# A Tile kernel on one core: high priority for the inverses of the triangular blocks and their merging

## The chip, the cores and the metric

The kernel runs on one core of one Trainium2 chip. The metric is the device time of one execution in microseconds; a kernel's time is the median of its runs. The engines are named as in the profile: PE is TensorE's matmul and PEld its weight load, DVE is VectorE, ACT is ScalarE, POOL is GpSimd, and SP is SyncE, which issues nearly all DMAs here.

## The reference

The reference is a trunk of two layers over 512 positions of width 1024. The first layer mixes tokens by an RWKV-7 recurrence, the second by a gated spatial unit, and a SwiGLU FFN stands behind each. The change touches the recurrence alone. For each of 16 heads of width 64 it is

```python
def step(S, inp):
    r_t, w_t, k_t, v_t, a_t, b_t = inp
    sa = jnp.einsum('bhij,bhj->bhi', S, a_t)
    S = (S * w_t[:, :, None, :]
         + sa[..., None] * b_t[:, :, None, :]
         + v_t[..., None] * k_t[:, :, None, :])
    y = jnp.einsum('bhij,bhj->bhi', S, r_t)
    return S, y
```

Its output y then goes through a norm per head, a bonus term, an output gate g and the product with w_o:

```python
    return (y * g) @ w_o
```

## The kernel before, in words

**The recurrence in chunks.** The 512 positions are cut into 8 chunks of 64. Within a chunk the steps depend on each other through a 64x64 lower triangular matrix per chunk and head, and the kernel inverts these matrices, so that a chunk becomes a few matrix products. The 16 heads are worked through in four blocks of four heads, called blocks 0 to 3. For each block b there are the steps

- E (`early`): decays, keys and gates; writes the operands to DRAM (sa, sb);
- F (`front`, L673 to L728): loads them back as ST and MV; PE forms the chunk products `lm` (L709); ACT and DVE copy their parts to LA (L715, the triangular matrices), MV (L712) and BX (L716); transposes `bkt` (L722) and four more copies to BX (L726, L727);
- B (`back`, L730 to L817), in which the change lies, described below;
- S (`scan`): for each chunk the state products `us` and `Yp` (L843, L856), the new state su on DVE and ACT (L847, L849), and loads of `su` on SP (L828);
- N (`finish`): the norm per head with mean mu (L879 to L901), the gates (L904 to L920) with loads g2 and g2r and the small DVE step g2x (L912), the transposes yt (L927), the product ob (L928), and the store of ob to `od` (L936) on SP, two for each of blocks 0 to 2.

**The step B.** First the inverses of the 32x32 diagonal blocks: LX is the transposed LA (L735, DVE), POOL masks LA in place (`LAs`, L738), and a recursion of 15 steps on DVE, each a product tm (L744) and an addition to Dm (L746), inverts 16x16 blocks. Steps are told apart below by the width of their tile: the seventh product is `128x2x63`, the eighth `128x128`, the ninth `128x2x63` again. Two DVE transposes give Dn and Dt (L749, L750). Then PE transposes MV to MVt (`mvt`, L751 to L760; ACT copies). Then the merging, first to 32x32 and then to 64x64: Qp (L766, PE, 64 small products of 32x32), Qs (DVE), Np and Tp (L775, L778, PE), copies of Np to Dn2 by ACT and of Tp to bdT by ACT and DVE (L783), Q2p (L789, PE), its copies to Q2 (L792 ACT, L793 DVE), T2p (L798, PE) and its copies to bdT (L802, ACT and DVE). Last, for each of four units, the product mp (L807, PE) with its ACT copy (L809), and two products gh (L814, PE), each with a pair of additions on DVE into MV (L816, L817).

**The end of the mixer.** The output product `acc` (L156 to L158, from `out_proj`) takes its left operand oT from ob: for k below 6 SP loads a pair of od back as `oraw` (L980), ACT rounds it to oT (L131) and DVE forms the rest (L132). Blocks 0 to 2 supply three such loads, and the first products acc are already run while block 3 is still in its step B.

**What sets the order.** The code is written in the order of PLAN (L33):

```python
PLAN = "P0 E0 P1 P2 E1 P3 E2 E3 X0 F0 B0 F1 V0 V1 V2 V3 B1 S0 F2 S1 F3 N0 B2 N1 B3 S2 N2 S3 N3".split()
```

so block 2's step B comes behind block 3's step F and block 0's step N. But that isn't the order in which an engine runs its instructions: the kernel is built with a scheduler (`schedule_with_timeline_sim=True`, L1135) that goes through the instructions with a modelled timeline and puts each engine's queue in order by priority, which without further words follows the code. It may pull an instruction forward where it models the engine as free. PSUM banks are shared by tags (`BANKS_RWKV`, L29), so an instruction that writes a bank waits until the former tile in it has been read; gh, Qp, Np, Tp, Q2p and T2p turn over the two banks of the tag `pt`.

Of the kernel before, what the change touches and what calls it, by code (L numbers as in the profile page):

```python
# [82 lines left out]
class Trunk:  # L83
# [287 lines left out]
    def rwkv(self, x0, nxt):  # L371
# [3 lines left out]
        with ExitStack() as ctx:  # L375
# [14 lines left out]
            def e2(name, shape=(P, 2, T), dt=F32):  # L390
                return rp.tile(list(shape), dt, name=name, tag="e2", bufs=E2)
# [338 lines left out]
            def back(b, o):  # L730

                MV, BX, LA, Dm = (o[n] for n in ("MV", "BX", "LA", "Dm"))
                LX = e2("LX", (P, 2, 528))

                v.transpose(full(LX), LA.rearrange("p q c (x t) -> p t (q c x)", x=2))  # L735
                LAu = LA.rearrange("p q c t -> p (q c) t")
                LAs = LA.rearrange("p q c (x t) -> p (q c) x t", t=16)
                g.tensor_tensor(LAs, LAs, m16.unsqueeze(1).unsqueeze(3).broadcast_to([P, 16, 4, 16]), op=ALU.mult)  # L738
                LXd, Dmd = diag(LX), diag(Dm)
                for j in range(15):  # L740
                    n = 15 - j
                    tm = rp.tile([P, 2, 64], F32, name="tm", tag="tm", bufs=1)
                    tv = tm[:, :, 0:n * (j + 1)].rearrange("p b (i c) -> p b i c", c=j + 1)
                    v.tensor_tensor(tv, LXd[:, :, j + 1:16, j:j + 1].broadcast_to([P, 2, n, j + 1]),  # L744
                                    Dmd[:, :, j:j + 1, 0:j + 1].broadcast_to([P, 2, n, j + 1]), op=ALU.mult)
                    v.tensor_tensor(Dmd[:, :, j + 1:16, 0:j + 1], Dmd[:, :, j + 1:16, 0:j + 1], tv, op=ALU.add)  # L746
                Dt = rp.tile([P, 16, 2, 32], F32, name="Dt", tag="hid", bufs=1)
                Dn = self.sm.tile([P, 16, 2, 32], F32, name="hn", tag="hn", bufs=2)
                v.transpose(Dn.rearrange("p u x s -> p s (u x)"), full(Dm).rearrange("p t s -> p s t"))  # L749
# [14 lines left out]
                for u in range(16):  # L764
                    for z, hd, x in quarters:
                        mm(Qp[z:z + 32, u * 32:(u + 1) * 32], LAu[z:z + 32, u, 32 * x:32 * x + 32], Dn[z:z + 32, u, x, :],  # L766
                           start=True, stop=True)
                Qs = el("Qs", (P, 16, 32))
                v.tensor_tensor(Qs, Qp.rearrange("p (u s) -> p u s", s=32), id32.unsqueeze(1).broadcast_to([P, 16, 32]), op=ALU.add)
                Np = self.bank("pt", "Np")  # L770
                Tp = self.bank("pt", "Tp")
                for u in range(16):
                    for z, hd, x in quarters:
                        if x == 0:
                            mm(Np[z:z + 32, u * 32:(u + 1) * 32], Dt[z:z + 32, u, x, :], Qs[z:z + 32, u, :], start=True, stop=True)  # L775
                for u in range(16):
                    for z, hd, x in quarters:
                        mm(Tp[z:z + 32, u * 32:(u + 1) * 32], Qs[z:z + 32, u, :], Dt[z:z + 32, u, x, :], start=True, stop=True)  # L778
                Dn2 = el("Dn2", (P, 16, 32))
                for z in (0, 64):  # L780
                    a.copy(Dn2[z:z + 32].rearrange("p u s -> p (u s)"), Np[z:z + 32, :])
# [357 lines left out]
```

## Time and profile before

| | |
|---|---|
| median of 3 runs | 1424.7 us (1423.27 to 1425.45) |
| the profiled execution | 1426.41 us, its span 1424.7 us |
| granted clock of PE, mean | 0.962 |
| busy share of PE, DVE, ACT, POOL | 94%, 56%, 40%, 19% |
| instructions | 21481 |
| DMA | 143.04 MB, mean 100 GB/s |

The span is the profiled execution from its first instruction to its last; all times below count from its start. PE is busy 94% of it. The page cuts the span in 40 slices of some 36 us, and the slices that are less full are at the start and around slices 5, 9 and 12 (180 to 470 us), where the recurrence is. The profile's line numbers are those of the kernel before; in the changed kernel they are 1 higher from L735 to L760 and 2 higher from L762 on.

### The profile page before, as it was taken

To read this page: it belongs to the slowest core of one execution; us is meant where nothing else is said; L and a number is where in the kernel's file an instruction comes from. 1 tells how busy PE (TensorE), PEld (TensorE's weight loads), DVE (VectorE), ACT (ScalarE), POOL (GpSimd) and SP (SyncE) were. 2 spreads that over 40 slices of the span, in tenths; PEclk is the share of its full clock that TensorE was granted. 3 is DMA by queue.
4 is the path that set the end of the run, shared out by engine and by line. 5 is a ranking of instruction groups with operands and counts; after the bars stand their busy time and mean duration, and the time that the engine had idled before them with its cause. 6 is when DMAs were issued, how large, how long until landed. Compare 5 with 4: busy or idle time off the path is not lost.

```text
span 1424.7 us, 21481 instructions
## 1 busy us (share of the span) xinstructions
PE 1338.3 (94%) x8472; PEld 1091.2 (77%) x8472; DVE 791.8 (56%) x1318; ACT 569.1 (40%) x1060; POOL 274.5 (19%) x248
## 2 busy tenths in 40 slices
PE   5899997987889979999999999999999999999998
PEld 3576686976768768888888888778888888888886
DVE  6962776388685775554544222865575455443223
ACT  5654665363723363323322122743363232322221
POOL 6154463133311231111111000210121111110000
PEclk9999998987969989999999999999999999999999
DMA  5133467351322423333332232343213333332331
GB/s 157 30 107 92 127 182 200 94 150 43 87 65 88 130 90 104 89 89 103 90 99 94 89 118 74 104 129 109 89 52 112 103 89 89 103 90 103 89 96 67
DMA packets 210324, 143.04 MB, mean 100 GB/s; under 512 B 59664, under 2 KB 185136, under 8 KB 210224
## 3 DMA queue, kind: packets, MB, share of 16 engines
q1 hardware_dynamic: 208544, 135.90, 32.2%
q0 software_dynamic: 1680, 5.77, 1.3%
q8 instruction: 67, 1.10, 0.3%
q14 instruction: 33, 0.27, 0.1%
HBM read 125.39 MB, written 14.16 MB: 98 GB/s over the span
## 4 chain that ended last, share of the span: by engine, by line
PE 77%; DVE 7%; ACT 2%; issue 2%; DMA 2%; POOL 1%; SPq 1%; DVEq 0%; POOLq 0%; ACTq 0%
PE gu L158 12%; PE gu L156 12%; PE gu L157 12%; PE acc L156 8%; PE acc L157 8%; PE acc L158 8%; PE gh L814 2%; PE lm L709 2%; PE u L156 1%; PE u L158 1%; PE u L157 1%; PE Yp L856 1%; PE mp L807 1%; PE proj L158 1%; PE proj L156 1%
## 5 line engine op out<-in xcount | busy, mean ns | idle before, releaser
L131 ACT CAST whi<-wraw 128x1024 fp32r<-128x1024 f32 x161 | 168.8, 1050 | 472.5 <-PE gu L157 257.2
L132 DVE TENSOR_TENSOR wlo<-wraw,whi 128x1024 fp32r<-128x1024 f32 x161 | 246.6, 1532 | 197.2 <-ACT whi L131 193.2
L157 PE MATMUL gu<-hT,whi 128*128 128x512 f32 (+1 forms) x768 | 289.6, 378 | 4.4 <-DVE hT L59 4.4
L156 PE MATMUL gu<-hT,whi 128*128 128x512 f32 (+1 forms) x768 | 290.2, 380 | 0.8 <-ACT hT L57 0.8
L158 PE MATMUL gu<-hT,wlo 128*128 128x512 f32 (+1 forms) x768 | 289.7, 378 | 0.0
L157 PEld LDWEIGHTS gu<-hT,whi 128*128 128x128 f32 x768 | 146.0, 190 | 34.0 <-DVE hT L59 4.7
L156 PEld LDWEIGHTS gu<-hT,whi 128*128 128x128 f32 x768 | 145.8, 191 | 29.5 <-ACT hT L57 1.0
L158 PEld LDWEIGHTS gu<-hT,wlo 128*128 128x128 f32 x768 | 145.8, 190 | 29.0 <-issue 0.2
L157 PE MATMUL acc<-wlo,act 128*128 128x512 f32 x416 | 163.9, 394 | 0.0
L156 PE MATMUL acc<-whi,act 128*128 128x512 f32 x416 | 163.6, 394 | 0.0
L158 PE MATMUL acc<-whi,act 128*128 128x512 f32 x416 | 160.5, 394 | 0.0
L333 POOL TENSOR_TENSOR sg<-sg,hn 128x512 f32<-128x512 f32 x44 | 56.7, 1288 | 422.5 <-DVE sg L332 422.5
L332 DVE TENSOR_TENSOR sg<-sg,gu 128x512 f32<-128x512 f32 x44 | 30.2, 687 | 142.5 <-PE gu L158 141.1
L148 POOL TENSOR_TENSOR wlo<-wraw,whi 128x1024 fp32r<-128x1024 f32 x28 | 70.1, 2505 | 169.9 <-ACT whi L147 151.1
L158 PEld LDWEIGHTS acc<-whi,act 128*128 128x128 f32 x416 | 78.2, 188 | 18.1
L156 PEld LDWEIGHTS acc<-whi,act 128*128 128x128 f32 x416 | 78.2, 188 | 18.0
L157 PEld LDWEIGHTS acc<-wlo,act 128*128 128x128 f32 x416 | 78.1, 188 | 18.0
L330 DVE TENSOR_TENSOR sg<-gu,hn 128x512 f32<-128x512 f32 x44 | 30.4, 691 | 67.8 <-PE gu L158 67.6
L131 ACT CAST act<-sg 128x512 fp32r<-128x512 f32 x52 | 32.3, 622 | 72.2 <-POOL sg L333 58.1
L158 PE MATMUL proj<-xsp,wlo 128*128 128x512 f32 x128 | 53.7, 421 | 0.0
L156 PE MATMUL proj<-xsp,whi 128*128 128x512 f32 x128 | 51.9, 405 | 0.4 <-ACT k L529 0.4
L709 PE MATMUL lm<-MV,ST 128*128 128x128 f32 x256 | 41.6, 316 | 11.2 <-DMA ST<-sb 7.9
(305 smaller groups left out, 2248.8 us busy)
## 6 DMA issues: line engine op xcount, KB each, us to landing
wraw<-in_ffn_w_gate_dram SPq DMA_DIRECT2D x44, 512.0 KB, 3.6
wraw<-in_ffn_w_up_dram SPq DMA_DIRECT2D x44, 512.0 KB
wraw<-in_ffn_w_down_dram SPq DMA_DIRECT2D x44, 512.0 KB, 3.6
wraw<-in_rwkv_w_rkv_dram SPq DMA_DIRECT2D x24, 512.0 KB, 3.5
wraw<-in_sgu_w_in_dram SPq DMA_DIRECT2D x16, 512.0 KB, 3.6
x<-in_x_dram SPq DMA_DIRECT2D x8, 512.0 KB, 3.7
MV<-sa SPq DMA_DIRECT2D x64, 64.0 KB, 2.6
ST<-sb SPq DMA_DIRECT2D x8, 512.0 KB, 4.5
```

The source lines that it names most:

```text
L131: self.nc.scalar.copy(hi, src)
L132: self.nc.vector.tensor_tensor(lo, src, hi.bitcast(F32), op=ALU.subtract)
L148: nc.gpsimd.tensor_tensor(lo, raw, hi.bitcast(F32), op=ALU.subtract)
L156: mm(out, lhs[0], rhs[0], start=start, stop=False)
L157: mm(out, lhs[0], rhs[1], start=False, stop=False)
L158: mm(out, lhs[1], rhs[0], start=False, stop=stop)
L330: nc.vector.tensor_tensor(sg, pp[0], yb, op=ALU.mult)
L332: nc.vector.tensor_tensor(sg, sg, pp[1], op=ALU.mult)
L333: nc.gpsimd.tensor_tensor(sg, sg, yb, op=ALU.mult)
L709: mm(lm[:, cc * P:(cc + 1) * P], st[:, cc].rearrange("p n t -> p (n t)"), mv[:, :, cc, hd, :], start=True, stop=True)
L807: mm(mp[:, cc * P:(cc + 1) * P], bdT[:, q * NC + 4 * hh + cc].rearrange("p h t -> p (h t)"), mt[:, cc, :], start=True, stop=True)
L814: mm(gh[:, cc * P:(cc + 1) * P], mt[rows, cc, :], bx[rows, 0:2, cc, :], start=True, stop=True)
```

## The change

The change wraps two parts of `back` in `with tc.high_priority():`, which tells the scheduler to place the instructions inside ahead of all that is ready outside. The first part runs from LX to the transposes Dn and Dt, the second from Qp to the copies of T2p. The transposes MVt between them stay outside, as do mp, gh and the additions behind them. Nothing is computed otherwise. The diff, without the lines that are only indented:

```diff
             def back(b, o):
 
                 MV, BX, LA, Dm = (o[n] for n in ("MV", "BX", "LA", "Dm"))
-                LX = e2("LX", (P, 2, 528))
-
-                v.transpose(full(LX), LA.rearrange("p q c (x t) -> p t (q c x)", x=2))
...
-                v.transpose(Dt.rearrange("p u x t -> p t (u x)"), full(Dm))
+                with tc.high_priority():
+                    LX = e2("LX", (P, 2, 528))
+
+                    v.transpose(full(LX), LA.rearrange("p q c (x t) -> p t (q c x)", x=2))
...
+                    v.transpose(Dt.rearrange("p u x t -> p t (u x)"), full(Dm))
                 MVt = {}
                 for hh in range(2):
...
-                quarters = [(64 * hd + 32 * x, hd, x) for hd in q2 for x in q2]
-                Qp = self.bank("pt", "Qp")
...
-                    cp(bdT[z:z + 32, :, hd, 32:64], T2p[z:z + 32, :].rearrange("p (u t) -> p u t", t=32))
+                with tc.high_priority():
+
+                    quarters = [(64 * hd + 32 * x, hd, x) for hd in q2 for x in q2]
+                    Qp = self.bank("pt", "Qp")
...
+                        cp(bdT[z:z + 32, :, hd, 32:64], T2p[z:z + 32, :].rearrange("p (u t) -> p u t", t=32))
 
                 for hh, q in units:
```

Each engine keeps the same number of instructions, and POOL the same order. On PE, DVE, ACT and SP the order changes in one place of the program, from block 2's merging to block 3's Q2p (360 to 434 us in the trace before); the steps B of blocks 0 and 1 keep theirs. Beside it three small transposes on PE change places with products of the FFN. On PE, block 2's Qp, Np, Tp, Q2p and T2p, which had been in pieces between `bkt`, `lm`, `us` and `Yp`, now run each in one piece or nearly so, T2p ahead of the last `lm` of block 3's step F (before, it ran behind it and behind the transposes mvt). Behind T2p PE then runs mvt x16, mp x4, mvt x8 and the first gh. The twelve first products acc stand ahead of block 3's Qp (before, between its Qp and Np). On ACT four copies of these tiles move ahead of the last copy to LA, and the last four copies of bkt as well.

On DVE the copy of T2p (to bdT_151) had stood in the midst of block 3's recursion (tm_4207 is its sixth product, Dm_3507 the tile it adds to; nr_ are small steps of block 1's norm). Before:

```order
L744 TENSOR_TENSOR tm_4207<-LX_4189,Dm_3507 128x2x60
L173 SCALAR_TENSOR_TENSOR nr_t_4127<-nr_t_4127,nr_a_4121 128x16
L802 COPY bdT_151<-T2p_3998 32x16x32
L746 TENSOR_TENSOR Dm_3507<-Dm_3507,tm_4207 128x2x10x6
L174 SCALAR_TENSOR_TENSOR nr_y_4125<-nr_t_4127,nr_y_4125 128x16
L744 TENSOR_TENSOR tm_4210<-LX_4189,Dm_3507 128x2x63
```

After, on the same engine, among the last parts of block 3's step F (MV<-lm) and block 1's states (su), and ahead of the mean mu of block 1's norm, which stands ahead of block 3's LX:

```order
L795 COPY Q2_3995<-Q2p_3962 32x512
L712 TENSOR_TENSOR MV_3483<-lm_3555,mk2_126 64x4x2x64
L847 TENSOR_TENSOR su_3437<-us_3440,pc_1044 64x2x64
L804 COPY bdT_151<-T2p_3998 32x16x32
L712 TENSOR_TENSOR MV_3492<-lm_3577,mk2_126 64x4x2x64
L712 TENSOR_TENSOR MV_3492<-lm_3586,mk2_126 64x4x2x64
L847 TENSOR_TENSOR su_3453<-us_3456,pc_1044 64x2x64
L712 TENSOR_TENSOR MV_3499<-lm_3608,mk2_126 64x4x2x64
L879 TENSOR_REDUCE mu_4113<-Y_3351 128x16
```

So the copy moves from the recursion to the stage ahead of it, where MV is still being filled.

The additions behind gh stand on DVE too, in the same recursion. Before, with tm_4222 its eleventh product of 15, and hn the sum behind block 1's norm:

```order
L744 TENSOR_TENSOR tm_4222<-LX_4189,Dm_3507 128x2x55
L746 TENSOR_TENSOR Dm_3507<-Dm_3507,tm_4222 128x2x5x11
L744 TENSOR_TENSOR tm_4225<-LX_4189,Dm_3507 128x2x48
L816 TENSOR_TENSOR MV_3191<-gh_4039,BX_3227 128x4x64
L817 TENSOR_TENSOR MV_3191<-gh_4039,MV_3191 128x4x64
L746 TENSOR_TENSOR Dm_3507<-Dm_3507,tm_4225 128x2x4x12
L901 TENSOR_TENSOR Y_3351<-Y_3351,hn_4138 128x1024
L744 TENSOR_TENSOR tm_4228<-LX_4189,Dm_3507 128x2x39
L816 TENSOR_TENSOR MV_3191<-gh_4046,BX_3227 128x4x64
L817 TENSOR_TENSOR MV_3191<-gh_4046,MV_3191 128x4x64
```

After, the first two pairs stand behind the product `128x128`, several steps earlier:

```order
L745 TENSOR_TENSOR tm_4213<-LX_4189,Dm_3507 128x128
L818 TENSOR_TENSOR MV_3191<-gh_4039,BX_3227 128x4x64
L819 TENSOR_TENSOR MV_3191<-gh_4039,MV_3191 128x4x64
L818 TENSOR_TENSOR MV_3191<-gh_4046,BX_3227 128x4x64
L819 TENSOR_TENSOR MV_3191<-gh_4046,MV_3191 128x4x64
L747 TENSOR_TENSOR Dm_3507<-Dm_3507,tm_4213 128x2x8x8
L903 TENSOR_TENSOR Y_3351<-Y_3351,hn_4138 128x1024
L745 TENSOR_TENSOR tm_4216<-LX_4189,Dm_3507 128x2x63
L132 TENSOR_TENSOR oT_5044<-oraw_5042,oT_5044 128x512
L818 TENSOR_TENSOR MV_3198<-gh_4059,BX_3258 128x4x64
L819 TENSOR_TENSOR MV_3198<-gh_4059,MV_3198 128x4x64
```

In all, seven of block 2's eight pairs now stand ahead of block 3's Dt, where three had stood.

On SP the loads and stores around block 1's two stores of od (ob_4166 and ob_4180) and the load oraw behind them change their order; su_ are loads for block 2's scan. Before:

```order
L936 DMA od_125<-ob_4166 128x512
L138 DMA wraw_5244<-in_rwkv_w_o_dram 128x2x512
L603 DMA g2_4894<-in_rwkv_g2_dram 128x256
L828 DMA su_4644<-Vd_116 64x2x64
L936 DMA od_125<-ob_4180 128x512
L828 DMA su_4644<-Vd_116 64x2x64
L909 DMA g2r_4900<-in_rwkv_g2_dram 32x256 x2
L828 DMA su_4660<-Vd_116 64x2x64 x2
L909 DMA g2r_4900<-in_rwkv_g2_dram 32x256
L980 DMA oraw_5080<-od_125 128x2x512
```

After:

```order
L938 DMA od_125<-ob_4166 128x512
L830 DMA su_4644<-Vd_116 64x2x64 x2
L603 DMA g2_4894<-in_rwkv_g2_dram 128x256
L830 DMA su_4660<-Vd_116 64x2x64 x2
L138 DMA wraw_5244<-in_rwkv_w_o_dram 128x2x512
L938 DMA od_125<-ob_4180 128x512
L911 DMA g2r_4900<-in_rwkv_g2_dram 32x256 x3
L982 DMA oraw_5080<-od_125 128x2x512
```

The loads of su now stand ahead of the second store, and only the three of g2r remain between it and oraw.

More of the change, by code (lines that the diff above doesn't have):

```diff
@@ L740, in back @@
[L740 to L746, printed above, removed]
@@ L760, in back @@
                         a.copy(mt[:, q].rearrange("p c f -> p (c f)"), pt)
-                quarters = [(64 * hd + 32 * x, hd, x) for hd in q2 for x in q2]
-                Qp = self.bank("pt", "Qp")
-                for u in range(16):
-                    for z, hd, x in quarters:
-                        mm(Qp[z:z + 32, u * 32:(u + 1) * 32], LAu[z:z + 32, u, 32 * x:32 * x + 32], Dn[z:z + 32, u, x, :],
-                           start=True, stop=True)
-                Qs = el("Qs", (P, 16, 32))
@@ L769, in back @@
[L769 to L778, printed above, removed]
@@ L791, in back @@
-                Q2 = el("Q2", (P, 16, 32))
-                a.copy(Q2[32:64].rearrange("p u s -> p (u s)"), Q2p[32:64, :])
-                v.tensor_copy(Q2[96:128].rearrange("p u s -> p (u s)"), Q2p[96:128, :])
-                T2p = self.bank("pt", "T2p")
-                for u in range(16):
-                    for hd in q2:
-                        z = 64 * hd
-                        mm(T2p[z:z + 32, u * 32:(u + 1) * 32], Q2[z + 32:z + 64, u, :], bdT[z + 32:z + 64, u, hd, 32:64],
-                           start=True, stop=True)
```

69 lines of the change are left out of this document (49 added, 20 removed).

## The prediction

> **What bounds the kernel now.** I read the page first, then the windows around the stage that the change touches, then what PE waits for there, then the timelines of PE, DVE, ACT and SP. In the page, the busy line of the whole span:
>
> ```profile
> PE 1338.3 (94%) x8472; PEld 1091.2 (77%) x8472; DVE 791.8 (56%) x1318; ACT 569.1 (40%) x1060; POOL 274.5 (19%) x248
> ```
>
> PE is the bound nearly everywhere, so only PE's idle or slow stretches can be won. Block 2's merging (Qp, Np, Tp, Q2p, T2p) up to block 3's Q2p lies between 360 and 436 us. The windows give for each stretch its length, then busy us of PE, PEld, DVE, ACT and POOL, the granted clock, and the DMA:
>
> ```profile
> 361.00:379.00 18.00, 18.00 (x359) 15.19 (x360) 5.84 (x11) 13.26 (x42) 2.56 (x5) 1.00 0.25 55
> 379.00:415.00 36.00, 24.97 (x277) 20.59 (x278) 35.50 (x69) 14.63 (x27) 13.45 (x8) 0.63 0.28 92
> 415.00:425.00 10.00, 10.00 (x94) 8.25 (x97) 4.86 (x14) 3.71 (x11) 0.00 (x0) 0.98 0.17 54
> 425.00:436.00 11.00, 9.18 (x427) 8.12 (x421) 4.38 (x9) 5.03 (x10) 0.00 (x0) 1.00 0.23 67
> 436.00:457.00 21.00, 20.74 (x255) 18.04 (x254) 10.75 (x28) 8.88 (x23) 0.93 (x3) 0.92 0.24 67
> ```
>
> So four stages follow each other: PE-bound (PE 18.00 of 18), then DVE-bound (35.50 of 36, PE idle for 11 us and at a clock of 0.63), then PE again with one last gap, then PE without end. The waits of PE from 379 to 436 us (us in total, times, longest) name the gap that the change aims at and the last one:
>
> ```profile
> PE mp L807 <- DVE bdT L802: 7.3, 1, 7.3
> PE Q2p L789 <- ACT bdT L783: 1.8, 1, 1.8
> ```
>
> **Which shift reaches the end.** Behind block 3's Q2p both kernels have the same order on PE, and PE is busy 20.74 of 21 us there. So what counts is when that Q2p starts. The chain of waits (start, us, what) shows what it hangs on:
>
> ```profile
> 425.88 4.80 DMA oraw<-od
> 430.70 0.63 ACT oT L131
> 434.16 1.20 PE Q2p L789 x63
> ```
>
> ACT has the two casts of oT ahead of the copies of Np that Q2p reads, in both orders; so Q2p comes 8.3 us (434.16 - 425.88) after the load of oraw is issued. That load reads what block 1's second ob has written. The rows of DVE and SP for these two, and two lines of the view of the tile od (ns of one issue as least, median and most, then the first and last start):
>
> ```profile
> 419.22 0.69 DVE L928 TENSOR_TENSOR ob<-yt,ob 128x512 f32<-128x512 f32 x1 [0.17 <-PE yt L927]
> 421.52 0.55 SPq L936 DMA_DIRECT2D od<-ob  x1
> L936 SPq DMA_DIRECT2D od<-ob x6: 320/344/547, 342.0 to 474.4; - x6
> L980 SPq DMA_DIRECT2D oraw<-od x3: 370/395/594, 380.2 to 478.1; - x3
> ```
>
> For the last pair, 474.4 and 478.1, oraw follows od by 3.7 us; in our place by 4.4, since loads of su stand between on SP. The term to find is therefore: when does the second ob finish in the new order?
>
> **The change part by part.**
>
> *The moved copies.* The copies of Tp, Q2p and T2p on DVE, and the row at which PE waits for the last:
>
> ```profile
> L783 DVE COPY bdT<-Tp 32x512 f32<-32x512 f32 x2 | 1.4, 680 | 0.0
> L793 DVE COPY Q<-Q2p 32x512 f32<-32x512 f32 x1 | 0.7, 698 | 0.0
> L802 DVE COPY bdT<-T2p 32x512 f32<-32x512 f32 x1 | 0.7, 689 | 0.0
> 396.22 0.69 DVE L802 COPY bdT<-T2p 32x512 f32<-32x512 f32 x1
> 396.96 2.07 PE L807 MATMUL mp<-MVt,bdT 128*128 128x128 f32 x8 [7.30 <-DVE bdT L802]
> ```
>
> They leave the DVE-bound stage for the PE-bound one, where DVE is busy 5.84 of 18 us and hides them: 1.4 + 0.7 + 0.7 = 2.8 us come off DVE's queue. The wait of 7.3 us as such ends. What is late next are the additions L816/L817 to the results of gh: in the new order the first of them still stand behind the step "128x128" of block 3's recursion, and the third gh needs the PSUM bank that they free. So PE waits there instead, and the gain is not 7.3.
>
> *The PE-bound stage grows.* Pieces of the merging on PE that stood behind or between the last lm of front 3, the transpose LX with which block 3's recursion begins, and ACT's copies of bkt:
>
> ```profile
> 378.25 0.69 PE L778 MATMUL Tp<-Dt,Qs 32*32 32x32 f32 x56
> 380.81 1.13 PE L789 MATMUL Q2p<-Dn,LA 32*32 32x32 f32 x58
> 388.46 1.20 PE L798 MATMUL T2p<-bdT,Q 32*32 32x32 f32 x64 [0.51 <-ACT bdT L783]
> L727 ACT COPY BX<-bkt 64x256 f32<-64x256 f32 x6 | 2.2, 366 | 0.1
> 380.16 1.95 DVE L735 STREAM_TRANSPOSE LX<-LA 128x1024 f32<-128x1024 f32 x1
> ```
>
> Now about half of Tp (0.7 of it here, as much again in other pieces), Q2p 1.1 and T2p 1.2 lie ahead of the last lm: up to 3.5 us more on PE. [...] ACT says the same as the upper end: it gets its four copies of these tiles ahead of the last LA, and four of bkt (4 x 0.37 = 1.5 us), which had come after it. I take +3.2, near the upper end since ACT is busy 13.26 of 18: LX starts at 383.4. Bounds 0 and 3.5.
>
> *DVE's queue from LX to the end of Dt.* Rows for its ends, for an addition pair, and for the work that changes sides:
>
> ```profile
> 403.87 0.42 DVE L816 TENSOR_TENSOR MV<-gh,BX 128x256 f32<-128x256 f32 x1
> 404.54 0.25 DVE L746 TENSOR_TENSOR Dm<-Dm,tm 128x96 f32<-128x96 f32 x1
> 414.29 0.43 DVE L816 TENSOR_TENSOR MV<-gh,BX 128x256 f32<-128x256 f32 x1
> 383.93 1.20 DVE L879 TENSOR_TENSOR Y<-Y,mu 128x1024 f32<-128x1024 f32 x1
> 418.37 0.68 DVE L132 TENSOR_TENSOR oT<-oraw,oT 128x512 fp32r<-128x512 f32 x1
> 415.36 0.41 DVE L912 TENSOR_TENSOR g2x<-g2r,g2x 32x256 fp32r<-32x256 f32 x1 [0.31 <-ACT g2x L911]
> ```
>
> From 380.16 to 414.29, where Dt has ended, are 34.1 us without idling. Out go the copies (2.8) and Y<-Y,mu with its small neighbour (1.3), now ahead of LX. In come four more addition pairs (three stood ahead of Dt, now seven; 404.54 - 403.87 = 0.67 each, 2.7), the second oT (0.7), g2x (0.4) and a su (0.3). Sum out 4.1, in 4.1: the queue is as long as before, and Dt ends at 383.4 + 34.1 = 417.5 if DVE never waits. Stalls of DVE while POOL works stay in it: a step of 0.28 us takes 2.40 while POOL multiplies Y, and POOL's order is unchanged.
>
> ```profile
> 399.89 2.40 DVE L746 TENSOR_TENSOR Dm<-Dm,tm 128x126 f32<-128x126 f32 x1
> 399.79 2.35 POOL L900 TENSOR_TENSOR Y<-Y,gn 128x1024 f32<-128x1024 f32 x1 [6.39 <-ACT MVt L809]
> ```
>
> *The added wait.* With seven pairs in the middle of the recursion, DVE waits in its queue for PE's gh, and the rest of the recursion, hn, Dt and the second ob wait behind it. It depends on the clock. gh at half and at full clock, and the clock after a gap:
>
> ```profile
> 407.60 3.09 PE L814 MATMUL gh<-BX,MVt 64*128 64x128 f32 x16
> 445.71 1.71 PE L814 MATMUL gh<-BX,MVt 64*128 64x128 f32 x16
> 410.00:415.00 5.00, 5.00 (x19) 3.81 (x18) 5.00 (x6) 2.22 (x5) 0.00 (x0) 0.50 0.30 110
> 415.00:420.00 5.00, 5.00 (x37) 4.20 (x37) 2.59 (x7) 1.74 (x5) 0.00 (x0) 0.95 0.09 30
> ```
>
> From the third gh to the end of the fourth PE has gh, mp, gh: at half clock 1.55 + 2.07 + 1.55 = 5.2 us. DVE has for that time a step, Y (1.2), a step, oT (0.7) and a pair, some 3.5: it waits 1.7. At full clock it is about half of 5.2, and nothing waits. PE will have been mostly idle from 381 to 399 and start at half clock. From 407.60 PE is never idle in the timeline, and still the clock is 0.50 until 415 and 0.95 on the mean of the next five: recovery took some 8 us. I take that, so one full wait and a little of the next: 2.0 us (bounds 0, at full clock, and 5, three such waits at half clock throughout). [...]
>
> *From Dt to Q2p.* Dt at 417.5 + 2.0 = 419.5; the last pair 0.7 and ob 0.7: 420.9; SP issues od at 421.0, as no su stands between od and its predecessors any more; oraw 3.7 later at 424.7, against 425.88: -1.2. PE has by then less left to do than before (the twelve products of acc stand ahead of Qp now, not behind it), so it idles some 6 us ahead of Q2p, not 1.8; after those 1.8 it ran acc at 0.63 us a matmul, after 439.4 at 0.39:
>
> ```profile
> 437.71 0.63 PE L156 MATMUL acc<-whi,oT 128*128 128x512 f32 x1
> 439.39 0.40 PE L157 MATMUL acc<-wlo,oT 128*128 128x512 f32 x1
> ```
>
> Some 3 us at half clock cost 1.6 now; after the longer gap they cost that and 0 to 1.7 more; I take 0.9. The sum: -1.2 + 0.9 = -0.3. Two of SP's moves (hn ahead of the weights, the third weight later) have only loads behind them that are needed much later; they and three places where PE orders transposes among gu products count nothing.
>
> The profiled execution took 1426.4 us with a span of 1424.7; the median of the runs is 1424.7, 1.7 below it. 1426.4 - 0.3 = 1426.1, as a median 1424.4.
>
> **The rivals.**
>
> 1. *The clock comes back early, and DVE never waits.* Dt at 417.5, oraw at 422.7, -3.2, and no extra cost ahead of Q2p: 1421.5. For it speaks that the third gap here (436 to 439) ended within some 3 us; against it the 8 us after the longer gap. If LX is less late than I think, the same comes out in another way. [...] Chance 0.26.
> 2. *Slower: half clock throughout the gh products.* Three waits, 5 us; Dt at 422.5, oraw at 427.7, +1.8, and 1.7 of extra half clock: +3.5, 1428.2. It decides from the point where DVE waits more than some 4 us in all for gh. For it: before, the clock stayed at half from the gap until 415. Chance 0.18.
> 3. *PE's instructions run out in the unbroken groups.* In block 1, whose Qp already is in one piece, PE stood 4.05 us in the midst of it, for nothing that the profile shows:
>
> ```profile
> 315.14 0.34 PE L766 MATMUL Qp<-hn,LA 32*32 32x32 f32 x9 [4.05 <-issue]
> ```
>
> If block 2's groups do that, LX comes 4 us later still: +3.7, 1428.4. Against it: block 3's Qp is in one piece as well and shows no pause. Chance 0.06.
>
> That the order doesn't change can be left out: blocks 0 and 1 stay as they were, but block 2's groups do move.
>
> **How the numbers follow.** A measurement of this kernel tells 0.2% (2.85 us) from no change. The forecast, within that, has 0.50; rival 1 is faster by more, 0.26; rivals 2 and 3 are slower by more, 0.24. The bounds of LX (-3.2, +0.3), the wait (-2, +3) and the clock (-0.9, +0.8) don't all go one way; together they make some 4 us either side, and half a microsecond more stands for the runs themselves, which lie 2.2 us apart (1423.27 to 1425.45). That is 1419.9 to 1428.9, which takes in all three rivals' middles and leaves out their tails.
>
> **What would show it.** Right: mp follows mvt without the 7.3 us wait, but PE waits some 5 us ahead of the third gh; LX some 3 us later; DVE's rows of the recursion idle for PE gh for about 2 us in all; second ob near 421 and oraw near 424.7; the same length behind Q2p. Wrong: LX at 380 or Dt ahead of 416 (then faster), or ob later than 423, or a pause of "issue" in Qp, Np or Tp (then slower), or work behind Q2p of another length.

## The result: 0.7% slower, as DVE now waits for products that PE runs at half clock

The changed kernel takes 1432.54 us, the median of six runs (1430.17 to 1440.13), against 1423.99 us of six runs before; the ratio is 1.0071, interval 1.0042 to 1.0101. The forecast was 1424.4 us with a range up to 1428.9. The profiled execution of the changed kernel took 1430.62 us with a span of 1428.9: 4.2 us more than the profiled one before, and near the lower end of its runs. Its lines from 735 on are 1 or 2 higher.

The page of the changed kernel, the busy line of the whole span:

```profile
PE 1334.5 (93%) x8472; PEld 1088.1 (76%) x8472; DVE 793.1 (56%) x1318; ACT 569.6 (40%) x1060; POOL 273.0 (19%) x248
```

PE does not work longer than before (1338.3): it works 3.8 us less and the span is 4.2 us longer, so the time is lost where PE idles, or waits for who waits for PE. What PE waits for from 355 to 445 us (us in total, times, longest; "issue" is a pause for which the profile shows no wait):

```profile
PE us L845 <- POOL Y L902: 6.7, 1, 6.7
PE Q2p L791 <- ACT Dn L783: 3.9, 2, 3.5
...
PE Q2p L791 <- issue: 1.5, 1, 1.5
PE Qp L768 <- issue: 0.8, 1, 0.8
```

The wait of 7.3 us for the copy of T2p is gone, as said. In its place stands one of 6.7, ahead of `us` and the third gh. The timeline of DVE of the same execution tells what is behind it, and gives the steps of the prediction:

```profile
387.40 1.98 DVE L736 STREAM_TRANSPOSE LX<-LA 128x1024 f32<-128x1024 f32 x1 [0.46 <-ACT LA L715]
...
402.35 2.43 DVE L745 TENSOR_TENSOR tm<-LX,Dm 128x128 f32<-128x128 f32 x1
404.70 0.41 DVE L818 TENSOR_TENSOR MV<-gh,BX 128x256 f32<-128x256 f32 x1
405.04 0.41 DVE L819 TENSOR_TENSOR MV<-gh,MV 128x256 f32<-128x256 f32 x1
...
412.37 0.42 DVE L818 TENSOR_TENSOR MV<-gh,BX 128x256 f32<-128x256 f32 x1 [3.05 <-PE gh L816]
...
417.31 0.42 DVE L818 TENSOR_TENSOR MV<-gh,BX 128x256 f32<-128x256 f32 x1 [1.81 <-PE gh L816]
...
426.09 2.04 DVE L751 STREAM_TRANSPOSE Dt<-Dm 128x1024 f32<-128x1024 f32 x1
...
428.61 0.69 DVE L930 TENSOR_TENSOR ob<-yt,ob 128x512 f32<-128x512 f32 x1
```

The first pair of additions stands behind the product `128x128`, and that takes 2.43 us here while POOL multiplies Y; the pair starts only at 404.70, and PE goes on at 405.2:

```profile
405.22 0.44 PE L845 MATMUL us<-su,MV 128*64 128x64 f32 x2 [6.74 <-POOL Y L902]
```

The profile names POOL's product of Y as what ended this wait, but `us` doesn't read Y. In the kernel it reads the part of MV that the first pair completes, and it starts 0.18 us behind the start of that pair's second addition (405.22 - 405.04), as the next `us` does behind the second pair's (405.88 - 405.70). So PE waits for DVE's pair, and the third gh stands behind `us` in PE's queue.

Then DVE waits in its turn for gh. The windows of the same execution say why (length, then busy us of PE, PEld, DVE, ACT and POOL, the granted clock, DMA):

```profile
400.00:405.00 5.00, 0.00 (x0) 0.00 (x0) 5.00 (x5) 0.00 (x0) 3.47 (x2) 0.74 0.25 70
405.00:416.00 11.00, 10.78 (x46) 9.28 (x46) 6.81 (x18) 3.75 (x6) 1.04 (x2) 0.50 0.21 61
416.00:420.00 4.00, 4.00 (x28) 3.19 (x28) 2.10 (x8) 1.10 (x3) 0.00 (x0) 1.00 0.02 7
```

In the gap the clock falls, and it stays at half for a further 11 us in which PE is busy nearly without end: rival 2's half clock. Eight products gh take 2.07 us in it (from 406.26) and 1.16 behind it (from 416.11). The end of the chain of waits:

```profile
429.33 2.81 DMA od<-ob
432.15 3.71 DMA oraw<-od
435.88 1.14 ACT oT L131 x2
...
438.14 1.92 PE Q2p L791 x64
```

Block 3's Q2p starts at 438.14, 4.0 us later than before (434.16). Behind it, the way to the start of the last gh of block 3 is 26.8 us (464.95 - 438.14), against 26.1 before (460.30 - 434.16).

One row over the whole stretch, from the first Qp of block 2 to the end of the last gh of block 3, makes the two kernels comparable. Before:

```profile
360.32:461.46 101.14, 88.03 (x1464) 74.23 (x1464) 65.87 (x137) 46.38 (x113) 20.15 (x19) 0.85 0.27 80
```

and after:

```profile
360.72:466.11 105.39, 86.80 (x1464) 74.40 (x1464) 65.87 (x136) 46.70 (x113) 19.52 (x19) 0.85 0.26 77
```

The stretch is 4.25 us longer, which is the whole difference of the two spans. PE's idle time in it is the length less PE's busy time: 13.1 us before, 18.6 after. The mean clock reads 0.85 in both, so some 30 us of each stretch, 2 x (1 - 0.85) of its length, run at half clock. The kernel before has its gap and its half clock too; what differs is where DVE waits for the products in it. Before, DVE doesn't wait for gh at all from LX to Dt. Its longest such wait comes behind Dt, ahead of the second ob:

```profile
417.70 0.42 DVE L816 TENSOR_TENSOR MV<-gh,BX 128x256 f32<-128x256 f32 x1 [1.93 <-PE gh L814]
```

In the changed kernel 5.45 us of these waits (3.05, 1.81 and 0.59) stand ahead of Dt, and the second ob comes behind all of them.

### The profile page after: what moved, and what is told of

The parts are those of the page before. It is cut to its first block, busy times and chain, and to the rows that moved or that the text cites. A ratio compares the mean times of both kernels' runs of the same rounds, so it can differ in the third digit from the quotient of the medians.

```text
span 1428.9 us, 21483 instructions
## 1 busy us (share of the span) xinstructions
PE 1334.5 (93%) x8472; PEld 1088.1 (76%) x8472; DVE 793.1 (56%) x1318; ACT 569.6 (40%) x1060; POOL 273.0 (19%) x248
## 4 chain that ended last, share of the span: by engine, by line
PE 76%; DVE 6%; ACT 3%; DMA 2%; issue 2%; POOL 1%; SPq 1%; DVEq 0%; POOLq 0%; ACTq 0%
PE gu L158 12%; PE gu L156 12%; PE gu L157 12%; PE acc L156 8%; PE acc L157 8%; PE acc L158 8%; PE gh L816 2%; PE mp L809 1%; PE u L156 1%; PE u L158 1%; PE u L157 1%; PE lm L709 1%; PE proj L158 1%; PE proj L156 1%; PE Yp L858 1%
```

## The experiments

Theory A: PE's gap, and the half clock behind it in which DVE waits for gh, are the loss. Theory B: the late LX alone is the loss, since block 3's recursion starts late and Q2p hangs on it. All ratios are to the kernel before, on the same chip.

### The changed kernel again, and its two parts

Nothing is edited in the first of these runs. The second keeps only the first `high_priority` (LX to Dt), the third only the second one, and that for block 2 alone:

```diff
-                with tc.high_priority():
+                with nullcontext():
                     LX = e2("LX", (P, 2, 528))
...
-                with tc.high_priority():
+                with tc.high_priority() if b == 2 else nullcontext():
 
                     quarters = [(64 * hd + 32 * x, hd, x) for hd in q2 for x in q2]
```

> The changed kernel once more, for a second profile. Its six runs went from 1430.2 to 1440.1 us, and the one profiled took 1430.6, at the lower end. Theory (a late tail and early pairs): the second profile shows the same places as the first, block 3's LX near 387 us and DVE waiting some 6 us for gh in the recursion; a run of 1434 us or more differs in how long PE's clock stays low after its idle time. Rival (something the first profile does not show): the places are the same in length, and a slower run loses its time behind 470 us.

> High priority for the first part alone (LX to Dn and Dt), the merging as before. Theory (the merging in one piece is the cause): as before, ratio 0.998 to 1.002, since almost nothing moves ahead of 425 us. Rival (the inverses' priority costs too): slower by 0.2% or more.

> High priority for the merging of block 2 alone. Theory: the whole loss is here, ratio 1.004 to 1.010 as in the changed kernel. Rival (the inverses' priority costs too): a ratio under 1.004.

The changed kernel took 1434.78 us in this one execution. The inverses alone give 1.0000 (0.9985 to 1.0016). The merging of block 2 alone gives 1.0063 (1.0039 to 1.0087): it carries the change's loss. The windows of the changed kernel's second profiled execution show what differs from its first:

```profile
396.50:404.00 7.50, 0.11 (x1) 0.01 (x1) 7.50 (x21) 0.59 (x1) 3.67 (x2) 0.73 0.16 57
404.00:423.50 19.50, 19.48 (x80) 16.12 (x80) 9.91 (x29) 5.83 (x11) 0.85 (x2) 0.50 0.12 32
423.50:428.00 4.50, 4.50 (x40) 3.80 (x40) 3.50 (x8) 1.46 (x4) 0.00 (x0) 0.96 0.17 47
```

Here PE's gap at `us` is 7.4 us, where it was 6.7, and PE then works at half clock for 19.5 us instead of 11. The stretch from block 2's first Qp to block 3's last gh is 111.70 us long (358.15 to 469.85) instead of 105.39, and the execution takes 4.2 us more. So the change costs 4.3 us in this stretch in one execution and 10.6 in the other (before, the stretch is 101.14 us long), and the loss between the medians, 8.6 us, lies between the two.

The six runs of the changed kernel lie 10 us apart, but 25 runs of the kernel before lie nearly as far apart (1420.13 to 1429.55), and block 2's first Qp, ahead of which the change moves nothing, starts anywhere from 355.59 to 363.22 us in the traces of these runs. A half clock of varying length is thus a part of the spread, and isn't shown to be all of it.

### The halves of the moved order

From here on the order of each engine is fixed by a table. Added to the kernel before is one function that adds edges of order, no waits, between consecutive instructions of an engine. Instructions stay the same unless said. Line numbers are 63 or 64 higher than before.

```diff
+def pin(tc):
+    traced = list(tc.nc.cur_bb.bb.instructions)
+    for steps in json.loads(zlib.decompress(base64.b85decode(ORDER))):
+        at, last = 0, None
+        for step in steps:
+            at += step
+            if last is not None:
+                tc.add_manual_dep(traced[at], traced[last].name, mybir.DependencyInfo(mybir.DependencyClass.NoSync, mybir.DependencyReason.DATA), reason="order")
+            last = at
...
         build(tc, ins, outs[0])
+        pin(tc)
```

The fourth run has the order after up to the end of block 3's step F, and the order before from there on:

```diff
-PE, DVE, ACT as before
+PE as after up to bkt_3627<-ident, then as before
+DVE as after up to MV_3499<-lm_3617, then as before
+ACT as after up to BX_3605<-lm_3617, then as before
```

> Each engine runs the changed kernel's order up to the end of block 3's step F, and from there the order of before. LX comes late as in the changed kernel, and the additions behind gh stand where they stood before. Theory (late LX and early pairs, each with its share): LX at 385 to 387 us, 6 later than before; DVE's queue from LX to Dt shorter by the copies (2.8), so Dt 3 us later, no waits for gh, and 1427 us, ratio 1.002. Rival (the late LX alone carries the loss): ratio 1.004 to 1.007. Rival (only the early pairs cost): as before or faster, 0.998 to 1.000.

It gave 1.0043 (1.0024 to 1.0062). LX came at 387.65, as after, Q2p at 439.57. The waits of its PE, however, hold a gap as well:

```profile
PE gh L877 <- ACT MVt L872: 8.7, 2, 8.4
```

So the run fits theory B but doesn't single it out. The fifth run is the other half, the order before with DVE's pairs at the places that they have after:

```diff
 tm_4213<-LX_4189,Dm_3507
+MV_3191<-gh_4039,BX_3227
+MV_3191<-gh_4039,MV_3191
+MV_3191<-gh_4046,BX_3227
+MV_3191<-gh_4046,MV_3191
...
 tm_4225<-LX_4189,Dm_3507
-MV_3191<-gh_4039,BX_3227
-MV_3191<-gh_4039,MV_3191
```

> The order of before on every engine, but on DVE two pairs of additions behind gh stand behind the product 128x128 and two more four steps later, near where the changed kernel has them. Theory (late LX first, early pairs second): LX stays at 380 us, DVE waits some 3 to 4 us for gh at half clock, Dt and the second ob come 2 to 4 us later, ratio 1.001 to 1.003. Rival (early pairs cost as much as the whole loss): 1.004 and more. Rival (early pairs cost nothing): 0.999 to 1.001, Dt where it was.

It gave 1.0065 (1.0041 to 1.0089) though block 2's merging stands where it stood before, and LX comes 19.8 us behind block 2's Qp as before. The expected size was missed. PE still waits 7.4 us at mp; the pairs now come up before gh is done, and DVE waits for it:

```profile
399.43 0.42 DVE L879 TENSOR_TENSOR MV<-gh,BX 128x256 f32<-128x256 f32 x1 [3.68 <-PE gh L877]
...
410.00 0.43 DVE L879 TENSOR_TENSOR MV<-gh,BX 128x256 f32<-128x256 f32 x1 [3.12 <-PE gh L877]
...
423.26 0.69 DVE L991 TENSOR_TENSOR ob<-yt,ob 128x512 f32<-128x512 f32 x1 [1.38 <-PE yt L990]
```

So 0.65% can be lost without a late LX; theory B alone doesn't hold. The sixth run is the reverse, the order after with DVE's order before from LX on:

```diff
 tm_4213<-LX_4189,Dm_3507
-MV_3191<-gh_4039,BX_3227
-MV_3191<-gh_4039,MV_3191
...
 tm_4225<-LX_4189,Dm_3507
+MV_3191<-gh_4039,BX_3227
+MV_3191<-gh_4039,MV_3191
```

> The order of the changed kernel, but behind LX the DVE runs the order of before, so that three pairs of additions stand ahead of Dt and not seven. Theory (late LX first, early pairs second): LX stays at 387 us, the waits for gh ahead of Dt go from 6 to 8 us down to 2, Dt ends near 421 us and not near 429, ratio 1.003 to 1.005. Rival (the late LX alone): ratio as in the changed kernel, 1.006 to 1.007, since the second ob waits for PE anyway.

It gave 1.0108 (1.0085 to 1.0132), the worst of all, and not what was expected: `us` on PE now waits 10.0 and 2.6 us, and the clock is at half from 401 to 438.8. DVE no longer waits for gh ahead of Dt, but 6.5 and 5.1 us for yt, ahead of the two ob. The place of the pairs on DVE and the order of PE belong together; the order of PE without that of DVE makes a longer gap, and so this run tells nothing on LX by itself.

### The trains of small products

The seventh run puts lm between Np and Tp of block 2 and bkt between Tp and Q2p, so that PE has other work where it paused. A train here is a group of small products that PE runs in one piece:

```diff
 PE: Np_3857<-Qs,Dt x64
+lm_3555<-MV,ST x8
 Tp_3858<-Dt,Qs x128
+bkt_3565<-ident,ST x4
 Q2p_3962<-Dn,LA x64
```

> The order of the changed kernel, but one group of lm and one of bkt stand on PE between Np and Tp and between Tp and Q2p, with the copies of that lm earlier on ACT and DVE. Theory A (LX is late in part because PE stands in its trains of small products, with nothing else between them, and falls to half clock after it): no pause in Q2p, LX at 384 us, 3 earlier than in the changed kernel, ratio 1.004. Theory B (only the work moved ahead of the last lm makes LX late): LX stays at 387 us and the ratio at 1.006 to 1.007.

LX comes 25.05 us behind Qp (383.91 - 358.86), where it was 26.68 after (387.40 - 360.72) and 19.84 before (380.16 - 360.32). The pause of 1.46 us in Q2p is gone, though one of 1.14 us now stands in Tp; the gap is not gone (`us` waits 7.7 us). The ratio is 1.0053 (1.0033 to 1.0074), whose interval overlaps that of the change: LX 1.6 us earlier brought back no part of the loss that the runs can show.

### The waits of the kernel before, one at a time

The eighth run takes only DVE's copy of T2p from its place in the recursion, ten places ahead. The tenth puts oraw directly behind od on SP. The eleventh has both.

```diff
 DVE: nr_a_4121<-va_4119
+bdT_151<-T2p_3998
...
 nr_t_4127<-nr_t_4127,nr_a_4121
-bdT_151<-T2p_3998
...
 SP: od_125<-ob_4180
+oraw_5080<-od_125
...
 g2r_4900<-in_rwkv_g2_dram
-oraw_5080<-od_125
```

> The order of before, and only DVE's copy of T2p to bdT stands ten places earlier, behind the first step of block 1's norm. PE's wait of 7.3 us for it falls below 2. Theory (the wait was cover of the DVE-bound stage): Dt and the second ob stay where they were, ratio 0.999 to 1.001. Rival (the wait itself costs, which the change's idea rests on): faster by 3 us or more, ratio 0.998 and below.

> The order of before, and only the third load oraw stands on SP directly behind the store of block 1's second ob, ahead of four loads of su and three of g2r. If Q2p of block 3 hangs on oraw, as in the sum of the prediction: oraw 1 to 1.5 us earlier, PE's wait of 1.8 us ahead of Q2p goes and half clock behind it with it, ratio 0.998 to 0.9995. Rival (PE's own queue is the limit there): 1.000.

> The order of before with both moves: DVE's copy of T2p ten places earlier, and the load oraw directly behind its od. Theory: the two add up, since the copy brings the second ob forward and the load shortens what is behind it, ratio 0.9965 to 0.998. Rival (one of them takes what the other gives): 0.998 to 0.999, as the copy alone.

They gave 0.9983 (0.9969 to 0.9998), 1.0010 (0.9997 to 1.0022) and 0.9985 (0.9970 to 0.9999): the two moves together give what the copy alone gives. In the eighth the wait at mp falls from 7.3 us to 1.4, and a wait at gh takes its place; the timeline of PE:

```profile
390.80 1.61 PE L870 MATMUL mp<-MVt,bdT 128*128 128x128 f32 x8 [1.40 <-DVE bdT L865]
400.05 3.10 PE L877 MATMUL gh<-BX,MVt 64*128 64x128 f32 x16 [7.64 <-ACT MVt L872]
```

ACT's copy of MVt stands behind a cast of weights whose load lands at 398. Its small gain goes with the clock, which is back at 405 here and not at 415.5: the second ob comes 36.3 us behind LX (416.19 - 379.88) instead of 39.1 (419.22 - 380.16). The tenth run falls against the prediction: oraw is issued 1.5 us earlier, and Q2p starts at 434.46, as late as before. Its chain of waits shows what Q2p hangs on instead:

```profile
431.62 1.12 PE Tp L841 x79
...
432.77 0.69 DVE bdT L846
433.48 0.58 ACT bdT L846
...
434.46 1.20 PE Q2p L852 x63
```

Q2p hangs on PE's own Np and Tp and the copies behind them there, while the load of oraw has room. The fourteenth and fifteenth run take away the following waits too: ACT's copy of MVt goes ahead of that cast of weights (both), and DVE's first four pairs go to places where gh should be ready, with ACT's second copy of MVt early as well and PE's four transposes yt behind the next gh (the fifteenth):

```diff
 ACT: bdT_151<-T2p_3998
+MVt_3764<-mp_4033
+MVt_3764<-mp_4053
 whi_5216<-wraw_5214
-MVt_3764<-mp_4033
...
-MVt_3764<-mp_4053
...
 DVE: Dm_3507<-Dm_3507,tm_4207
+MV_3191<-gh_4039,BX_3227
+MV_3191<-gh_4039,MV_3191
+MV_3191<-gh_4046,BX_3227
+MV_3191<-gh_4046,MV_3191
...
```

> The kernel before, with two copies moved: DVE's copy of block 2's T2p ten places ahead, and ACT's copy of MVt from mp ahead of the cast whi that waits for a load of weights. Theory (a wait that is taken away comes back at the next reader of the same bank as long as DVE's additions stand where they are): the 7.3 us at mp and the 7.6 us at gh both go, and PE waits 4 to 8 us at the third gh for the additions instead; ratio 0.997 to 1.000, as with the DVE copy alone. Rival (the gap closes for good, the clock stays up): ratio 0.993 to 0.996.

> As the kernel with both copies early, and with the first four pairs of additions on DVE at the places where gh should be ready (the first two right behind the third step after the start of the recursion, one step of the norm behind them, two more pairs behind the next steps), and ACT's second copy of MVt early. LX isn't moved. Theory (the late LX and the gap in PE are the whole loss of the change): no gap over 3 us on PE between 380 and 405, the clock not at half for more than 7 us there, Q2p at 426 to 430, ratio 0.992 to 0.997. Rival (each pair moved ahead delays block 3's recursion by its own time and a wait, and Q2p hangs on the recursion): Dt 2 us later or more, ratio 0.999 to 1.004.

They gave 0.9986 (0.9972 to 0.9999) and 0.9990 (0.9975 to 1.0005). In the fourteenth the gap came back as one of 4.1 us, as expected. The fifteenth has no gap over 2.1 us, but it brought none of the gain that theory A expected; two of its windows:

```profile
382.00:385.00 3.00, 1.31 (x18) 0.89 (x10) 3.00 (x6) 2.94 (x8) 2.58 (x1) 1.00 0.36 130
385.00:419.50 34.50, 28.18 (x180) 23.55 (x180) 30.61 (x66) 10.64 (x19) 10.12 (x7) 0.51 0.24 81
```

Behind several short idle pieces, 1.7 us in three, the clock falls at 385 and stays at half for 34 us. (In the kernel before it falls at 384.7 too, but is back at 388.2 until the large gap.) Closing the one large gap is not enough; the half clock came without it.

### The gap filled with work

If the half clock is the loss, useless work in the gap should win it back. Transposes of the identity are added on PE (work is added, none left out): 36 in the changed kernel's gap in the ninth run, 24 in the gap of the eleventh kernel in the twelfth, then 62 in the changed kernel (thirteenth), in the kernel before (sixteenth) and in the eleventh kernel (seventeenth), and 62 in the seventh kernel (eighteenth). In each the table puts them where PE waits.

```diff
                 for q, ob in enumerate(gates(b)):
+                    if b == 1 and q == 0:
+                        warm = self.bank("pf", "warm")
+                        for n in range(62):
+                            nc.tensor.transpose(warm[:, n % 4 * P:n % 4 * P + P], self.ident, self.ident)
                     gated(b, Y, q, ob, tts)
```

> The order of the changed kernel, with 36 transposes of the identity into a free PSUM bank on PE in the place where it waits 6.7 us ahead of the third gh (work added, nothing left out). Theory (half clock after the gap makes DVE wait for gh, and its varying length spreads the runs): the clock stays at 1 from 398 us on, gh and mp in the recursion take 1.2 us per group and not 2.1, DVE's waits for gh ahead of Dt fall from 6 to 9 us to under 2, the second ob comes 4 us earlier or more, ratio 1.001 to 1.004, runs within 6 us of each other. Rival (the late LX carries the loss whatever the clock does): ratio 1.005 or more.

> As the run with both moves, with 24 transposes of the identity on PE in its wait between the first mp and the first gh. If the half clock after that gap costs: clock at 1 before 403 us, another 1 to 2 us off, ratio 0.995 to 0.997. Rival (the added transposes run at half clock themselves and end behind the gap): as without them or 1 us slower.

> The changed kernel, with 62 transposes of the identity on PE in the place where it waits 6.7 us for the third gh's bank (36 took 4.09 us and left 3.3 us open; 62 should take about 7.0). Work is added, none left out. Theory (the loss is PE's idle gap and the half clock behind it): the clock stays at full from 397 on, DVE waits under 2 us for gh in place of some 6, Dt near 422, ratio to before 0.999 to 1.004. Rival (the late LX alone makes the loss, the clock adds nothing): the clock stays up and the ratio is still 1.005 to 1.008.

> The kernel before, with 62 transposes of the identity on PE right behind block 2's T2p, where it waits 7.3 us for DVE's copy. Work is added, none left out. Theory (an idle gap costs mainly by the half clock that follows it, in both kernels): no half clock from 388 on up to the last gap ahead of block 3's Q2p, DVE's waits for gh gone, second ob 1 to 3 us earlier, ratio 0.994 to 0.998. Rival (the kernel before hangs on DVE's recursion, not on PE's clock): the clock stays up and the ratio is 0.999 to 1.001.

> The kernel with T2p's copy early and oraw directly behind od, with 62 transposes in the wait of 7.4 us for ACT's MVt copy, where 24 left 3.46 us open and the clock fell. Theory: with the gap closed the clock stays up from 396 on, ratio to before 0.993 to 0.997, the best of these kernels. Rival (the time hangs on DVE's recursion): ratio 0.998 to 1.000, as without the transposes.

> The changed kernel with both mendings at once: lm between Np and Tp and bkt between Tp and Q2p, so that PE's groups of small products are no longer in one piece (alone 1.0053), and 62 transposes in the 6.7 us gap (alone 1.0004). Theory (the pauses and the gap are separate terms): the two gains add, LX near 385, ratio 0.997 to 1.000. Rival (LX's earlier start is lost again at Q2p): ratio 1.000 to 1.002.

The ninth gave 1.0060 (1.0043 to 1.0076), the twelfth 0.9999 (0.9984 to 1.0014): both had too few transposes. In the ninth 36 take 4.09 us and leave 2.45 us open, in the twelfth 24 leave 3.5 us open, and the clock fell at 403.8 and 402.7. The twelfth decided nothing. The ninth shows that the loss doesn't go by the length of the gap: the idle time ahead of `us` is down from 6.7 to 2.45 us, but the half clock follows all the same, and the ratio stays up. The expectation's rival had named this ratio for a clock that stays up, which it doesn't here:

```profile
404.00:420.50 16.50, 16.50 (x67) 13.65 (x67) 7.83 (x24) 4.43 (x9) 0.00 (x0) 0.50 0.10 29
```

The thirteenth, which differs from the ninth only in the number of transposes, gave 1.0004 (0.9985 to 1.0023). Its PE in the gap:

```profile
399.97 6.93 PE L1001 MATMUL warm<-ident 128*128 128x128 f32 x62
```

and its windows around and behind it:

```profile
400.00:407.00 7.00, 6.95 (x65) 6.74 (x64) 7.00 (x17) 0.59 (x1) 3.76 (x2) 1.00 0.23 65
407.00:424.00 17.00, 16.95 (x125) 14.03 (x126) 14.80 (x37) 7.58 (x15) 0.78 (x2) 1.00 0.18 50
```

The clock stays up from 400 to 424 us. LX is as late as in the change (389.24, 26.9 us behind Qp), and no useful product runs earlier in the gap; still the ratio falls from 1.0071 (and from 1.0060 with 36 transposes) to 1.0004, and its interval meets neither of the others. DVE's waits for gh from 355 to 445 us (us in total, times, longest) in the kernel before, in the changed kernel, and with the gap filled (there from 350 us on):

```profile
DVE MV L816 <- PE gh L814: 4.0, 5, 1.9
DVE MV L818 <- PE gh L816: 5.9, 4, 3.1
DVE MV L879 <- PE gh L877: 2.2, 4, 0.7
```

Of the first none lies between LX and Dt, of the second 5.45 us, of the third 1.7. Dt starts 34.1 us behind LX (423.30 - 389.24) instead of 38.7 (426.09 - 387.40), and the stretch from block 2's first Qp to block 3's last gh takes 102.07 us (362.36 to 464.43), against 105.39 and 111.70 in the changed kernel and 101.14 before. This profiled execution as a whole (1430.02 us) is hardly shorter than the first one of the changed kernel (1430.62): its Qp starts 1.6 us later and 1.0 us more lies outside its span, so the comparison of the times rests on the medians.

This is the run that bears theory A out: with the clock up, 0.67 of the 0.71% are gone. The idle time itself is still taken, by the transposes, so it is the half clock behind it, through the waits on DVE, that cost the time.

The sixteenth gave 0.9983 (0.9967 to 1.0000), just above the range expected: the kernel before pays for its own half clock too, but only some 0.17%, and the interval reaches to nothing. DVE's wait of 1.93 us behind Dt is gone in it, and the second ob comes 36.9 us behind LX (417.10 - 380.25) instead of 39.1. With both gaps filled, the changed kernel stands at 1.0004 / 0.9983 = 1.0021 of the kernel before. That is the best value for what the late LX and the trains cost by themselves; the two intervals overlap, so it may be nothing. The seventeenth gave 0.9975 (0.9958 to 0.9991), 1421.39 us, also just above its expected range, and the best of all kernels here. The stretch from block 2's first Qp to block 3's last gh is 98.1 us long in it:

```profile
359.38:457.49 98.11, 89.88 (x1526) 77.33 (x1526) 65.29 (x136) 46.42 (x113) 20.33 (x19) 0.93 0.28 80
```

That is a mean clock of 0.93, not 0.85, and 8.2 us idle.

The eighteenth was expected at 0.997 to 1.000 and gave 1.0022 (0.9996 to 1.0048): its ten runs lie between 1420.89 and 1436.21, far apart, and its profiled one took 1434.46. There the gap was filled, and the clock still fell a little later:

```profile
396.50:403.00 6.50, 6.50 (x62) 6.50 (x61) 6.50 (x20) 1.21 (x2) 2.83 (x1) 1.00 0.04 10
403.00:406.00 3.00, 2.07 (x17) 1.56 (x15) 3.00 (x7) 1.22 (x2) 1.71 (x3) 1.00 0.59 186
406.00:423.00 17.00, 17.00 (x70) 13.80 (x69) 8.42 (x27) 4.61 (x10) 0.00 (x0) 0.51 0.09 26
```

Some 0.9 us of idle time in three, behind the transposes, went ahead of the fall, and then 17 us of work without a pause ran at half clock. The other nine runs weren't traced, so whether they met this isn't shown; what decides how long it lasts is open.

## Why the prediction was wrong

**The wait that takes the place of the removed one: right in place and near in size.** mp follows without its 7.3 us, and PE waits 6.7 us ahead of `us` and the third gh, where 5 had been said. What PE waits for is the first pair, as said, but for the MV that `us` reads, and not for a bank.

**LX: the first step that failed.** It was to be 3.2 us later, with bounds 0 and 3.5, and came 7.2 us later (387.40 against 380.16), 0.4 of it because block 2's Qp came later. The upper bound was made from the pieces of PE work that move ahead, and left out that PE stops in such trains: "issue" of 0.85 us in Qp and 1.46 us in Q2p, and the wait of 0.44 for Dn. For the lower bound of 0 no run shows a saving: counted from block 2's Qp, LX came 6.8 us later in the changed kernel (26.68 - 19.84) and 5.2 in the seventh run (25.05 - 19.84). The seventh run gives 1.6 us back by putting other products between the trains. The other 2.0 us beyond the forecast weren't taken apart by a run. By itself the late LX costs little: the thirteenth run has it too and stands at 1.0004.

**DVE's queue: right in length, wrong in waits.** From LX to the end of Dt are 40.7 us (426.09 + 2.04 - 387.40); without 5.95 us of waits for gh and yt (3.05, 0.50, 1.81 and 0.59, of which the longest two are shown above) that is 34.8, and 34.1 was forecast. The added wait was set at 2.0 us with a bound of 5 and measured 5.95. This is the step that made the time: I took a recovery of the clock in some 8 us, and PE worked at half clock for 11 in one execution and 19.5 in another. The 8 us had been counted from 407.60, but in that trace the clock was at half from 391.6 on, with PE busy for 15.2 of 16.5 us from 399 on. In the thirteenth run, with the clock up, Dt came 4.6 us sooner behind LX, which is the size of the miss.

**od, oraw, Q2p: wrong in its reason, and near in size by luck.** oraw follows od by 2.8 us (3.7 said). The 8.3 us from oraw to Q2p were read from an execution in which Q2p hung on the copies of Np and Tp; the tenth run shows this. In the changed kernel, where oraw does bind, the way is 6.0 us (438.14 - 432.15): 2.3 us to the good, 1.1 of it because the load itself took 3.71 us and not 4.80. Behind Q2p the change costs 0.7, forecast 0.9.

**The sum.** Q2p was forecast at 433.0 (424.7 + 8.3). To this add 4.0 for LX, 4.6 for the stretch to the end of Dt (40.7 against 36.1), less 0.3 from Dt's end to od, 0.9 from od to oraw and 2.3 from there to Q2p, and it is 438.1. The two misses of some 4 us make 8.6; three smaller ones, which happened to go the other way, took 3.5 us of it back. The medians differ by twice as much as the profiled executions (8.6 us against 4.2); the second execution of the changed kernel, with the longer half clock, took 4.2 us more than the first.

**The rivals.** Rival 1 (the clock comes back early) did not come: once the clock had fallen in the gap, it came back only at 416, though PE was busy from 405 on (10.78 of 11 us at 0.50 in the row 405 to 416 above); it stayed up only where the gap was filled. Rival 2 (half clock throughout) is what happened, at a chance of 0.18; its price of 3.5 us was below the change's loss of 8.6 us, since it kept LX at +3.2 and set the waits at 5. Rival 3 (pauses) happened in part, with 0.85 and 1.46 us instead of 4. The three were reckoned as separate cases; here two came together, and both were slower. That, and bounds for LX that allowed for no waiting, made the range too narrow.

## What to carry to other kernels

Taking a wait away in a chain of four engines moved it to the next link here, in the changed kernel and in the eighth and fourteenth run: follow each reader of the same tile or bank to the end before you count the gain. Before you let another engine read PE's products sooner, price them at half clock for as long as the longest stretch at half clock in the trace (23.9 us in the kernel before): holding the clock up was worth some 0.17% in the kernel before, where DVE waits for gh only behind Dt, and 0.67% in the changed one, where it waits in the midst of the recursion. The orders of engines that feed each other should be judged together: of this change's order, parts alone lost 0.4 to 1.1%, one of them more than the whole.

## What was not expected of the hardware

How long the clock stayed at half differed widely. Read in rows of 0.2 to 0.5 us, the stretch around the gap was 13.7 us long in the first execution of the changed kernel (402.4 to 416.0), and 23.9 in the second (400.0 to 423.9) and in the kernel before (391.6 to 415.5). In the fifteenth run, which had no large gap, it was 34.1 us (385.5 to 419.6). Two such stretches of the kernel before, the one around its gap and one in block 1 of some 17 us:

```profile
391.60:415.50 23.90, 17.22 (x78) 14.54 (x78) 23.22 (x53) 5.45 (x10) 5.26 (x4) 0.50 0.20 66
330.50:347.50 17.00, 11.14 (x48) 9.54 (x47) 14.22 (x38) 2.98 (x7) 4.49 (x5) 0.51 0.15 40
```

In the eighteenth run the clock stayed down for 17 us (406 to 423) with PE busy for all of them, and in the second execution of the changed kernel PE was busy for 19.48 of the 19.5 us. The fall in the eighteenth run followed a row in which PE was busy for 2.07 us of 3.00 (403 to 406). What decides how long the clock stays down was not found, nor tried with other kinds of products.
